# Output projection and second feed-forward product with tokens stationary and 512 weight columns moving

## The chip, the cores and the metric

The kernel runs on one core of one Trainium2 chip. The metric is device time in microseconds (us), the median of a few runs; 2190.91 us for the kernel before, over 3 runs from 2189.48 to 2193.85 us.

## What is computed

Two encoder layers over 256 tokens of 2048 numbers. Each layer runs an input projection, three mixers, an output projection and a feed-forward pair. The two products that the change touches are the one with `w_out` and the one with `w_ff2`:

```python
x = x + jnp.einsum('bse,ed->bsd', y, w_out)      # y: the mixers' outputs, 2048 wide
h = rms_norm(x, norm_ff)
u = jax.nn.relu(jnp.einsum('bsd,df->bsf', h, w_ff1))   # 8192 wide
return x + jnp.einsum('bsf,fd->bsd', u * u, w_ff2)
```

All of it is float32. The kernel keeps that precision on TensorE by cutting every operand in two parts, hi and lo, whose sum is the number, and by adding three products: hi by hi, hi by lo, lo by hi.

## The kernel before, in words

**Weights.** `Weights` (line 212) walks a fixed list of tiles of 128 partitions by 1024 numbers (512 KB). SyncE loads each into `wst` (3 buffers), ScalarE casts it into `whi`, VectorE subtracts to get `wlo` (4 buffers each). `next()` starts the cutting of a tile two tiles ahead of its use.

**Two forms of a large product.** `in_group` (line 362), the input projection, keeps tokens on the PSUM partitions: for each of 16 tiles of the inner dimension (kt) and each of the 2 token tiles (tt), a 128x128 block of the activations is stationary and 512 columns of the weights move, three matmuls of 512 columns. `w_half` (line 386), used for `w_out`, `w_ff1` and `w_ff2`, keeps the output columns on the PSUM partitions: for each kt and each block of 128 output columns, a block of `whi` is stationary while the activations' hi and lo halves (2 x 256 columns side by side) move, and then a block of `wlo` is stationary while the hi half alone moves: one matmul of 512 columns and one of 256.

```python
            mm(c, ps, wh, acts[k0 + k], first and k == 0, end)
            mm(c, ps[:, :S], wl, acts[k0 + k][:, :S], False, False)
```

Below, a *unit* is one kt, 128 tokens and 512 output columns. In the first form it is three matmuls of 512 columns. In the second form a pair (512 and 256 columns) serves 128 output columns of all 256 tokens, half as many outputs as a unit, so a unit is two pairs: four matmuls. Either way 1536 columns move.

**Residual and norms.** `c.x` holds the residual transposed, as 16 tiles of 128 columns by 256 tokens. `out_end` (1005) adds a product's block to it; `ff2_end` (1084) multiplies by the tokens' factor `r2` first. `new_xg` (339) makes from such a tile the next product's operand `xg` (hi on ScalarE, lo on VectorE) and sums squares on GpSimd into `acc`; `square_factor` and `token_factor` sum `acc` over partitions with a small matmul (`ff_r`, `stat`).

**Stages of a layer.** Nine groups of the input projection with the mixers' steps between them; `out_proj` (1015): the first four blocks of columns over the first half of `y`, then over the second, and then the other twelve; four chunks of the feed-forward pair (`ffn`, 1048): 16 blocks of `w_ff1` give 16 tiles `u`, then 16 blocks of `w_ff2` add into x.

**What sets the order.** Each engine runs its instructions in the order in which the Python code issues them. `Stream` (113) keeps a model clock; the mixers' and the ends' steps are generators that `pump()` resumes between two matmuls, when the model says that their operands are there. PSUM has 4 banks for the large products (`g`) and 4 for the rest (`m`). A transpose is a matmul against the identity (line 196).

Of the kernel before, what the change touches and what calls it, by code (L numbers as in the profile page):

```python
# [45 lines left out]
# columns of a layer's vectors  # L46
# [17 lines left out]
# where the MLA heads start: group and weight tile of the input projection  # L64
# [4 lines left out]
class Engine:  # L69
    """An engine's instructions, with an estimate of the time (us) that each one takes."""  # L70
# [141 lines left out]
class Weights:  # L212
    """Weight tiles in the order of their use: loaded and split ahead of it."""
# [13 lines left out]
    def split(self):  # L227
        """hi + lo = w exactly, both in float32r."""
# [27 lines left out]
def weight_order(c, depth):  # L256
    srcs = []
    for l in range(depth):
# [7 lines left out]
        for half in range(2):  # L266
            for i in range(4):
                srcs.append((c.w_out[l, i, half], 1024))
        for i in range(4, KT):
            for half in range(2):  # L270
                srcs.append((c.w_out[l, i, half], 1024))
        for ch in range(NCHUNK):
            for w in (c.w_ff1[l, ch * KT:(ch + 1) * KT], c.w_ff2[l, ch]):
                for i in range(KT):
                    for half in range(2):
                        srcs.append((w[i, half], 1024))
# [11 lines left out]
def rsqrt(c, v, n):  # L288
    """1/sqrt of v [128, n] (n small): exp(-ln(v)/2) and a Newton step."""
# [38 lines left out]
def mm3(c, out, l, r, start, stop):  # L328
    """(l hi + l lo)^T (r hi + r lo) without lo * lo."""
# [9 lines left out]
def new_xg(c, xg, kt, gain):  # L339
    """The next product's operand from x tile kt, and its squares' sum."""  # L340
    nc = c.nc
    hl = tile_xg(c)
    nc.scalar.activation(hl[:, :S], c.x[kt], AF.Copy, scale=gain)
    if kt == 0:
        c.acc = c.small.tile([P, S], F32, tag="acc", name="acc", bufs=1)
        nc.gpsimd.tensor_tensor(out=c.acc, in0=c.x[kt], in1=c.x[kt], op=ALU.mult)
    else:
        sq = c.tmp.tile([P, S], F32, tag="sq", name="sq", bufs=1)
        nc.gpsimd.tensor_tensor(out=sq, in0=c.x[kt], in1=c.x[kt], op=ALU.mult)
# [3 lines left out]
    nc.vector.scalar_tensor_tensor(out=hl[:, S:], in0=c.x[kt], scalar=gain, in1=hl[:, :S].bitcast(F32),  # L353
                                   op0=ALU.mult, op1=ALU.subtract)
    xg[kt] = hl

# [5 lines left out]
def in_group(c, w, hooks=None, prepare=None):  # L362
    """x @ w_in columns: tokens on partitions, [128, w] for each token tile."""
    ps = [c.gps.tile([P, 512], F32, tag="g", name="g") for _ in range(NT)]
    for kp in range(KT // 2):
# [3 lines left out]
        for j in range(2):  # L369
            kt = 2 * kp + j  # L370
            c.s.until(lambda: c.xg[kt])
            wh, wl = hi[:, j * w:(j + 1) * w], lo[:, j * w:(j + 1) * w]
            for tt in range(NT):
                xh = c.xg[kt][:, tt * P:(tt + 1) * P]
                xl = c.xg[kt][:, S + tt * P:S + (tt + 1) * P]
# [25 lines left out]
def token_factor(c, rt):  # L401
    """rsqrt(mean(x^2) + eps) and its negative for each token: [128, 2 * NT]."""
    nc = c.nc
    ps = yield from bank(c, "stat")
    for tt in range(NT):
        mm(c, ps[:, 2 * tt:2 * tt + 2], c.acc[:, tt * P:(tt + 1) * P], c.mean[:, :2], True, True)
    v = c.small.tile([P, 2], F32, tag="tf_v", name="tf_v")
    yield
    nc.vector.tensor_scalar(out=v, in0=ps[:, 0:4:2], scalar1=EPS, scalar2=None, op0=ALU.add)
    c.s.give(m=1)  # L410
# [16 lines left out]
def layer_tables(c):  # L427
    """Rope tables with the layer's gains in them."""
# [18 lines left out]
def latents(c, ps, rt, tf):  # L447
    """Normalised query and key/value latents, transposed and split."""
# [38 lines left out]
def apply_rope(c, out, x, cos, sin, n, rot):  # L487
    """out = x*cos + swap(x)*sin; x, out [128, n, rot] views, tables [128, n, rot]."""
# [11 lines left out]
def k_rope(c, z1):  # L500
# [17 lines left out]
    # hi twice, for a query's hi and lo one above the other, and lo  # L518
# [10 lines left out]
def softmax(c, sc, scale, bias):  # L529
    """softmax(scale * (sc + bias)), keys on partitions, split; sc [128, NT, S] in PSUM."""  # L530
# [50 lines left out]
def mla_head(c, h):  # L581
# [22 lines left out]
    # per token: q nope, k nope, q rope  # L604
# [57 lines left out]
def dil_prep(c, ps, rt, pair):  # L662
    """Two dilated heads, normalised and rotated: columns q0 q1 k0 k1."""
# [62 lines left out]
def ml_gates(c, z1):  # L726
    """Decay sums F, inputs i - F and their running maxima for both directions."""
# [8 lines left out]
    # log_sigmoid(f) = min(f, 0) - log1p(exp(-|f|)); log1p(e) = 2 atanh(e / (2 + e)), a series in (1/3)^2  # L736
# [49 lines left out]
    # rows of hi and lo parts, which the selector adds exactly  # L786
# [19 lines left out]
def ml_qk(c, ps, rt):  # L806
# [7 lines left out]
    for pr in range(2):  # L814
# [6 lines left out]
        # per head: k's hi and lo one above the other, q's hi twice, and q's lo  # L821
# [28 lines left out]
def ml_o(c, ps, rt):  # L850
    """sigmoid(o) times the output norm's gain."""
# [19 lines left out]
def ml_head(c, h):  # L871
# [86 lines left out]
def mixers(c, prepare):  # L958
# [21 lines left out]
    s.spawn(ml_gates(c, z1))  # L980

# [23 lines left out]
def out_end(c, ps, mb, nxt):  # L1005
    nc = c.nc
    yield
    t = c.tmp.tile([P, S], F32, tag="ev1", name="ev1", bufs=3)
    nc.vector.tensor_tensor(out=t, in0=ps[:, S:], in1=c.x[mb], op=ALU.add)
    nc.vector.tensor_tensor(out=c.x[mb], in0=ps[:, :S], in1=t, op=ALU.add)  # L1010
    yield
    yield from new_xg(c, nxt, mb, c.vec[:, V_GF + mb:V_GF + mb + 1])


def out_proj(c):
    nxt = [None] * KT
    G = 4
    ps = [c.gps.tile([P, 512], F32, tag="g", name="g") for _ in range(G)]
    for h in range(2):
        for i in range(G):  # L1020
            w_half(c, c.y, 8 * h, ps[i], h == 0, h == 1)
            if h == 1:
                c.s.spawn(out_end(c, ps[i], i, nxt))
    for mb in range(G, KT):
        p = c.gps.tile([P, 512], F32, tag="g", name="g")
        for h in range(2):
            w_half(c, c.y, 8 * h, p, h == 0, h == 1)
        c.s.spawn(out_end(c, p, mb, nxt))
# [3 lines left out]
def square_factor(c, begin):
    """r^2 = 1 / (mean(x^2) + eps), the same on all partitions."""
    nc = c.nc
    c.r2 = c.small.tile([P, S], F32, tag="r2", name="r2", bufs=1)
    while c.s.clk < begin:
        yield
    ps = yield from bank(c, "ff_r")
    mm(c, ps[:, :S], c.mean, c.acc, True, True)
    yield  # L1040
    nc.vector.tensor_scalar(out=c.r2, in0=ps[:, :S], scalar1=EPS, scalar2=None, op0=ALU.add)
    c.s.give(m=1)
    for h in range(2):
        yield
        nc.vector.reciprocal(c.r2[:, h * P:(h + 1) * P], c.r2[:, h * P:(h + 1) * P])


def ffn(c, l, last_layer):
    """relu(r z)^2 = r^2 relu(z)^2: the tokens' factor r^2 comes after the second product."""
    nc = c.nc  # L1050
    nxt = [None] * KT
    c.s.spawn(square_factor(c, c.s.clk + 12.0))
    for ch in range(NCHUNK):
# [30 lines left out]
def ff2_end(c, ps, db, l, ch, last_layer, nxt):  # L1084
    nc = c.nc
    yield
    t = c.tmp.tile([P, S], F32, tag="ev1", name="ev1", bufs=3)
    nc.scalar.copy(t, ps[:, S:])
    yield
# [12 lines left out]
    yield from new_xg(c, nxt, db, c.vec[:, V_GM + db:V_GM + db + 1])  # L1102
# [190 lines left out]
```

## Time and profile before

| | |
|---|---|
| median of 3 runs | 2190.91 us (2189.48 to 2193.85) |
| span of the profiled execution | 2186.4 us |
| outside the span, against that median | 4.5 us |
| TensorE busy | 99% of the span |
| VectorE, ScalarE, GpSimd busy | 68%, 50%, 10% |
| HBM traffic | 177 GB/s over the span |

The page of the profiled execution gives its span, from the first instruction to the last, and no time of its own beside it; the 4.5 us is the difference to the runs' median. A matmul's recorded duration runs to its modelled end and overlaps the next one's, so what a matmul costs in a stream is the distance from its start to the next start, or a stretch divided by the count of matmuls in it.

### The profile page before, as it was taken

The numbers are of one execution on the slowest core, as the hardware profiler recorded it, in microseconds if no ns is written. First come the engines' busy times: TensorE is split into PE (matmuls) and PEld (weight loads), VectorE is DVE, ScalarE is ACT, GpSimd is POOL, SyncE is SP. The second block draws the span as 40 slices with busy tenths as digits, with TensorE's granted clock in tenths as the row PEclk, the third lists the DMA queues.
The fourth block names the chain that finished last, engine by engine and source line by source line (L and its number), as shares of the span: only waits on it lengthen the run. The fifth ranks groups of instructions, "written<-read, shape, count | busy, mean of one in ns | idle before, by whom it ended". The sixth has DMA issues, their size and how long they took to land.

```text
span 2186.4 us, 31853 instructions
## 1 busy us (share of the span) xinstructions
PE 2156.9 (99%) x12040; PEld 1861.3 (85%) x12040; DVE 1489.3 (68%) x2330; ACT 1100.4 (50%) x1953; POOL 218.5 (10%) x235
## 2 busy tenths in 40 slices
PE   8999999999999999999999999999999999999999
PEld 6788888888888888888887888888888888888887
DVE  7767777666666666667866687776666666666665
ACT  5666654544444444454556666444444444444443
POOL 6112123000000000002411121330000000000000
PEclk9999999999999999999999999999999999999999
DMA  6443445555555555555554334555555555555554
GB/s 229 151 141 119 157 168 185 192 191 184 187 188 186 189 184 191 185 184 199 185 165 158 122 116 164 174 192 192 184 184 192 184 187 188 188 188 185 191 190 157
DMA packets 109882, 387.98 MB, mean 177 GB/s; under 512 B 12448, under 2 KB 14624, under 8 KB 109728
## 3 DMA queue, kind: packets, MB, share of 16 engines
q1 hardware_dynamic: 106848, 382.88, 51.4%
q10 hardware_dynamic: 2880, 3.07, 0.4%
q8 instruction: 94, 1.54, 0.3%
q14 instruction: 60, 0.49, 0.1%
HBM read 383.80 MB, written 2.10 MB: 177 GB/s over the span
## 4 chain that ended last, share of the span: by engine, by line
PE 92%; ACT 3%; POOL 2%; DVE 2%; issue 1%; DMA 0%; POOLq 0%; ACTq 0%
PE g L190 86%; PE mla_z L190 1%; PE mla_s L190 1%; ACT junk L94 1%; POOL acc L94 1%; ACT whi L94 1%; PE oT L190 1%; POOL sq L94 1%; PE ml_h L190 1%; DVE wlo L94 0%; PE ml_st L190 0%; PE pT L196 0%; PE dil_s L190 0%; POOL rp L94 0%; PE dqkT L196 0%
## 5 line engine op out<-in xcount | busy, mean ns | idle before, releaser
L94 DVE TENSOR_TENSOR wlo<-wst,whi 128x1024 fp32r<-128x1024 f32 (+2 forms) x732 | 910.8, 1248 | 255.4 <-ACT whi L94 246.6
L94 ACT CAST whi<-wst 128x1024 fp32r<-128x1024 f32 (+2 forms) x732 | 758.6, 1041 | 371.3 <-PE g L190 292.6
L190 PE MATMUL g<-xg,whi 128*128 128x512 f32 x2048 | 714.5, 398 | 0.0
L190 PE MATMUL g<-u,whi 128*128 128x512 f32 x2048 | 711.0, 394 | 0.0
L190 PE MATMUL g<-u,wlo 128*128 128x256 f32 x2048 | 557.2, 282 | 0.0
L190 PE MATMUL g<-xg,wlo 128*128 128x256 f32 x2048 | 554.2, 281 | 0.0
L190 PEld LDWEIGHTS g<-xg,whi 128*128 128x128 f32 x2048 | 376.7, 188 | 82.5
L190 PEld LDWEIGHTS g<-u,whi 128*128 128x128 f32 x2048 | 376.5, 188 | 77.7
L190 PEld LDWEIGHTS g<-xg,wlo 128*128 128x128 f32 x2048 | 386.6, 189 | 12.6
L190 PEld LDWEIGHTS g<-u,wlo 128*128 128x128 f32 x2048 | 384.9, 188 | 12.4
L190 PE MATMUL g<-whi,xg 128*128 128x512 f32 (+1 forms) x1152 | 373.2, 391 | 6.5 <-ACT whi L94 6.5
L94 ACT COPY ev<-g 128x256 f32<-128x256 f32 x256 | 95.3, 372 | 474.7 <-PE g L190 474.7
L94 DVE TENSOR_TENSOR ev<-g,ev 128x256 f32<-128x256 f32 x256 | 108.6, 424 | 245.9 <-ACT ev L94 245.8
L190 PEld LDWEIGHTS g<-whi,xg 128*128 128x128 f32 x1152 | 215.6, 189 | 45.9 <-ACT whi L94 6.5
L190 PE MATMUL g<-wlo,xg 128*128 128x512 f32 (+1 forms) x576 | 221.9, 385 | 3.5 <-DVE wlo L94 3.3
L190 PE MATMUL g<-y,whi 128*128 128x512 f32 x512 | 178.4, 395 | 0.0
L190 PE MATMUL g<-y,wlo 128*128 128x256 f32 x512 | 139.3, 282 | 0.0
L190 PEld LDWEIGHTS g<-wlo,xg 128*128 128x128 f32 x576 | 109.1, 189 | 23.4 <-DVE wlo L94 6.9
L190 PEld LDWEIGHTS g<-y,whi 128*128 128x128 f32 x512 | 94.1, 188 | 19.3
L190 PEld LDWEIGHTS g<-y,wlo 128*128 128x128 f32 x512 | 96.3, 188 | 3.0
L94 POOL TENSOR_TENSOR sq<-x 128x256 f32<-128x256 f32 x60 | 78.2, 1303 | 126.4 <-DVE x L94 125.2
L94 ACT ACTIVATE xg<-x,vec 128x256 fp32r<-128x256 f32 x64 | 31.6, 508 | 86.8 <-DVE x L94 84.5
(199 smaller groups left out, 1353.2 us busy)
## 6 DMA issues: line engine op xcount, KB each, us to landing
wst<-w_ff SPq DMA_DIRECT2D x512, 512.0 KB, 3.2
wst<-w_in SPq DMA_DIRECT2D x128, 512.0 KB, 3.5
wst<-w_out SPq DMA_DIRECT2D x64, 512.0 KB, 3.2
wst<-w_in SPq DMA_DIRECT2D x16, 336.0 KB, 2.8
wst<-w_mla SPq DMA_DIRECT2D x12, 416.0 KB, 3.3
x<-xT SPq DMA_DIRECT2D x8, 256.0 KB, 5.3
out<-x ACTq DMA_DIRECT2D x16, 128.0 KB, 3.1
vec<-vecs ACTq DMA_DIRECT2D x2, 468.0 KB, 4.5
```

The lines of the kernel that those rows point to most:

```text
L94: return fn(*args, **kw)
L190: c.nc.tensor.matmul(out, lhsT, rhs, start=start, stop=stop)
```

## The change

`w_out` and `w_ff2` go over to the token-stationary form (`token_group`, made out of `in_group`); `w_ff1` stays in `w_half`. The residual is kept as 2 tiles of 128 tokens by 2048 columns. A group is now 512 columns of both token tiles in two PSUM banks, accumulated over all kt (the output projection's first two groups take the first half of `y` first). The end of a group is one VectorE operation for each token tile; in `ff2_end` the tokens' factor is a scalar per partition. `next_xg` takes the place of `new_xg`: ScalarE squares with a running sum, TensorE transposes each 128x128 block through a PSUM bank, and ScalarE and VectorE cut the result in hi and lo with the gain. The first norm still reads `xT`, now through borrowed buffers; the token-major copy of x (2 loads of 1 MB) is read behind the second group of the input projection. The output leaves in token order.

```diff
-def new_xg(c, xg, kt, gain):
+def next_xg(c, xg, g, ss, col):
+    nc = c.nc
+    for tt in range(NT):
+        j = c.tmp.tile([P, 512], F32, tag="junk5", name="junk5", bufs=1)
+        nc.scalar.activation(j, c.x[tt][:, g * 512:(g + 1) * 512], AF.Square, accum_out=ss[:, tt, g:g + 1])
+    for half in range(2):
+        kt = 4 * g + 2 * half
+        tp = yield from bank(c, "xT")
+        for i in range(2):
+            for tt in range(NT):
+                transpose(c, tp[:, i * S + tt * P:i * S + (tt + 1) * P], c.x[tt][:, (kt + i) * P:(kt + i + 1) * P])
+        yield
+        hls = [tile_xg(c) for i in range(2)]
+        split_gains(c, hls, tp, col + kt)
+        c.s.give(m=1)
+        xg[kt:kt + 2] = hls
+        yield
...
+def token_group(c, acts, ps, w, kps=range(KT // 2), hooks=None, prepare=None):
+    for kp in kps:
...
         hi, lo = c.w.next()
         for j in range(2):
             kt = 2 * kp + j
...
             for tt in range(NT):
...
                 mm(c, ps[tt][:, :w], xh, wh, kt == 0, False)
                 mm(c, ps[tt][:, :w], xh, wl, False, False)
                 mm(c, ps[tt][:, :w], xl, wh, False, kt == KT - 1)
...
 def mixers(c, prepare, after):
...
     s.spawn(ml_gates(c, z1))
+    if after:
+        after()
...
-def out_end(c, ps, mb, nxt):
+def out_end(c, ps, g, ss, nxt):
     nc = c.nc
+    cols = slice(g * 512, (g + 1) * 512)
     yield
-    t = c.tmp.tile([P, S], F32, tag="ev1", name="ev1", bufs=3)
-    nc.vector.tensor_tensor(out=t, in0=ps[:, S:], in1=c.x[mb], op=ALU.add)
-    nc.vector.tensor_tensor(out=c.x[mb], in0=ps[:, :S], in1=t, op=ALU.add)
+    for tt in range(NT):
+        nc.vector.tensor_tensor(out=c.x[tt][:, cols], in0=ps[tt], in1=c.x[tt][:, cols], op=ALU.add)
     yield
-    yield from new_xg(c, nxt, mb, c.vec[:, V_GF + mb:V_GF + mb + 1])
+    yield from next_xg(c, nxt, g, ss, V_GF)
...
-        for db in range(KT):
-            ps = c.gps.tile([P, 512], F32, tag="g", name="g")
-            for half in range(2):
-                w_half(c, us, 8 * half, ps, half == 0, half == 1)
-            c.s.spawn(ff2_end(c, ps, db, l, ch, last_layer, nxt))
+        for g in range(NX):
+            ps = two_banks(c)
+            token_group(c, us, ps, 512)
+            c.s.spawn(ff2_end(c, ps, g, l, ch, last_layer, nxt))
...
-    nc.scalar.copy(t, ps[:, S:])
-    yield
-    nc.vector.tensor_tensor(out=t, in0=ps[:, :S], in1=t, op=ALU.add)
-    nc.vector.tensor_tensor(out=t, in0=t, in1=c.r2, op=ALU.mult)
-    nc.vector.tensor_tensor(out=c.x[db], in0=c.x[db], in1=t, op=ALU.add)
+    for tt in range(NT):
+        nc.vector.scalar_tensor_tensor(out=c.x[tt][:, cols], in0=ps[tt], scalar=c.r2[:, tt:tt + 1],
+                                       in1=c.x[tt][:, cols], op0=ALU.mult, op1=ALU.add)
...
+    def load_tokens():
+        for tt in range(NT):
+            nc.sync.dma_start(c.x[tt], x[tt])
```

**How the order moves, first place.** TensorE at the start of the first chunk's second product, before the change (`g` is the PSUM bank, `u` the activations, `whi` and `wlo` the weights' parts; the operands are written in the program's order and not by which is stationary):

```order
L190 MATMUL g_4884<-u_4139,whi_4833 128x512
L190 MATMUL g_4884<-u_4139,wlo_4834 128x256
L190 MATMUL g_4884<-u_4192,whi_4833 128x512
L190 MATMUL g_4884<-u_4192,wlo_4834 128x256
L190 MATMUL g_4884<-u_4253,whi_4833 128x512
L190 MATMUL g_4884<-u_4253,wlo_4834 128x256
```

The same place with the change:

```order
L193 MATMUL g_4728<-whi_4677,u_3988 128x512
L193 MATMUL g_4728<-wlo_4678,u_3988 128x512
L193 MATMUL g_4728<-whi_4677,u_3988 128x512
L193 MATMUL g_4729<-whi_4677,u_3988 128x512
L193 MATMUL g_4729<-wlo_4678,u_3988 128x512
L193 MATMUL g_4729<-whi_4677,u_3988 128x512
L193 MATMUL g_4728<-whi_4677,u_4040 128x512
```

One `u` tile took a pair in each of sixteen blocks; it now takes six matmuls of 512 columns in each of four groups, three in either bank. Nothing stands between them.

**Second place.** TensorE with the change in the first product of the feed-forward pair, right behind the output projection of layer 0 (`xg_3917`, `xg_3918`, `xg_3935`, `xg_3936` are the operand's tiles kt 12 to 15, `xT` the bank of the transposes, `x_90` and `x_91` the residual):

```order
L193 MATMUL g_3871<-xg_3917,whi_3852 128x512
L193 MATMUL g_3871<-xg_3917,wlo_3853 128x256
L193 MATMUL g_3871<-xg_3918,whi_3852 128x512
L193 MATMUL g_3871<-xg_3918,wlo_3853 128x256
L199 MATMUL xT_3930<-const_92,x_90 128x128
L199 MATMUL xT_3930<-const_92,x_91 128x128
L199 MATMUL xT_3930<-const_92,x_90 128x128
L199 MATMUL xT_3930<-const_92,x_91 128x128
L193 MATMUL g_3871<-xg_3935,whi_3852 128x512
L193 MATMUL g_3871<-xg_3935,wlo_3853 128x256
L193 MATMUL g_3871<-xg_3936,wlo_3853 128x256
L193 MATMUL g_3871<-xg_3936,whi_3852 128x512
```

ScalarE at that place, from the last group's end on:

```order
L97 ACTIVATE junk5_3895,xss_3135<-x_90 128x512
L97 ACTIVATE junk5_3897,xss_3135<-x_91 128x512
L97 CAST whi_3906<-wst_3837 128x1024
L97 ACTIVATE xg_3917<-xT_3899,vec_88 128x256
L97 ACTIVATE xg_3918<-xT_3899,vec_88 128x256
L97 ACTIVATE xg_3935<-xT_3930,vec_88 128x256
L97 ACTIVATE xg_3936<-xT_3930,vec_88 128x256
```

Before the change these sixteen products stood in a row with no transposes among them. Now the last four transposes stand directly ahead of the matmuls that need their result; the four ahead of those (`xT_3899`) stand behind the first matmuls of kt 6.

**Third place.** SyncE with the change, at the third group of the input projection of layer 0:

```order
L227 DMA wst_522<-w_in 128x1024
L227 DMA wst_539<-w_in 128x1024
L227 DMA wst_569<-w_mla 128x832
L1208 DMA x_90<-x 128x2048
L1208 DMA x_91<-x 128x2048
L227 DMA wst_593<-w_in 128x1024
L227 DMA wst_644<-w_in 128x1024
```

The two loads of the residual stand between the first weights of an attention head and the fifth tile of that group.

## Rows read from the trace of the kernel before

**Rows 1.** The page: span, busy time by engine, granted clock in 40 slices.
```profile
span 2186.4 us, 31853 instructions
...
PE 2156.9 (99%) x12040; PEld 1861.3 (85%) x12040; DVE 1489.3 (68%) x2330; ACT 1100.4 (50%) x1953; POOL 218.5 (10%) x235
...
PEclk9999999999999999999999999999999999999999
```

**Rows 2.** The page, chain that ended last: share of the span by line.
```profile
PE g L190 86%; PE mla_z L190 1%; PE mla_s L190 1%; ACT junk L94 1%; POOL acc L94 1%; ACT whi L94 1%; PE oT L190 1%; POOL sq L94 1%; PE ml_h L190 1%; DVE wlo L94 0%; PE ml_st L190 0%; PE pT L196 0%; PE dil_s L190 0%; POOL rp L94 0%; PE dqkT L196 0%
```

**Rows 3.** TensorE's waits in the whole span: total us, times, longest us.
```profile
PE g L190 <- DVE wlo L94: 3.3, 6, 0.8
```

**Rows 4.** Chain, three stretches (w_ff2, w_out, input projection): start, us, what, instructions.
```profile
477.94 82.10 PE g L190 x467
...
299.78 80.35 PE g L190 x457
...
1098.82 20.19 PE g L190 x89
```

**Rows 5.** Timeline of TensorE in the w_ff2 product: start us, us, instruction.
```profile
530.12 0.39 PE L190 MATMUL g<-u,whi 128*128 128x512 f32 x1
530.35 0.28 PE L190 MATMUL g<-u,wlo 128*128 128x256 f32 x1
530.47 0.39 PE L190 MATMUL g<-u,whi 128*128 128x512 f32 x1
```

**Rows 6.** Timeline of TensorE, four transposes between matmuls of the input projection.
```profile
83.16 0.40 PE L190 MATMUL g<-whi,xg 128*128 128x512 f32 x1
83.40 0.60 PE L196 MATMUL nkT<-const,nk 128*128 128x128 f32 x4
...
84.07 0.39 PE L190 MATMUL g<-wlo,xg 128*128 128x512 f32 x1
```

**Rows 7.** Timeline of TensorE around the small matmul of square_factor.
```profile
389.48 0.28 PE L190 MATMUL g<-xg,wlo 128*128 128x256 f32 x1
...
390.25 0.28 PE L190 MATMUL g<-xg,wlo 128*128 128x256 f32 x1
```

**Rows 8.** Groups by form, whole span: count, busy us, mean ns, idle before.
```profile
L94 DVE TENSOR_TENSOR wlo<-wst,whi 128x1024 fp32r<-128x1024 f32 x704 | 884.5, 1259 | 243.8 <-ACT whi L94 235.2
L94 ACT CAST whi<-wst 128x1024 fp32r<-128x1024 f32 x704 | 736.0, 1050 | 349.3 <-PE g L190 279.4 <-DMA wst<-w_in 26.4 <-DVE x L94 26.1
...
L94 DVE TENSOR_TENSOR p_lo<-pT,p_hi 128x512 fp32r<-128x512 f32 x24 | 16.2, 681 | 18.4 <-ACT p_hi L94 18.4
...
L94 ACT ACTIVATE dil_z<-g,rt 128x512 f32<-128x512 f32 x12 | 7.7, 699 | 0.0
...
L196 PE MATMUL nkT<-const,nk 128*128 128x128 f32 x48 | 7.2, 272 | 0.0
...
L94 DVE SCALAR_TENSOR_TENSOR mla_k<-nkT,vec,mla_k 128x256 fp32r<-128x256 f32 x12 | 5.7, 475 | 0.0
L94 ACT ACTIVATE mla_k<-nkT,vec 128x256 fp32r<-128x256 f32 x12 | 5.7, 474 | 0.0
```

**Rows 9.** DMA at its fullest; then SyncE's and ScalarE's timelines near 60 us.
```profile
22.00:26.00 4.00, 3.58 (x16) 2.28 (x14) 4.00 (x5) 1.05 (x1) 3.77 (x4) 1.00 0.97 388
...
53.58 0.33 SPq L224 DMA_DIRECT2D wst<-w_mla  x1
57.46 0.33 SPq L224 DMA_DIRECT2D wst<-w_in  x1
...
60.93 1.05 ACT L94 CAST whi<-wst 128x1024 fp32r<-128x1024 f32 x1 [1.74 <-DMA wst<-w_in]
```

**Rows 10.** The last pieces of the chain, then the page's weight loads.
```profile
2181.90 0.38 ACT ev L94
...
2183.22 0.43 DVE x L94
...
wst<-w_ff SPq DMA_DIRECT2D x512, 512.0 KB, 3.2
```

More of the change, by code (lines that the diff above doesn't have):

```diff
@@ L34 @@
 NG = 8
+NX = D // 512
+OUT_ORDER = [(g, range(4 * h, 4 * h + 4)) for h in range(2) for g in range(2)] + [(g, range(8)) for g in (2, 3)]
 C_ID, C_MEAN, C_ONE, C_TRIU, C_TRIL = (i * P for i in range(5))
@@ L265, in weight_order @@
                 srcs += [(c.w_mla[l, h], 832) for h, at in enumerate(MLA_AT) if at == (g, kp)]
-        for half in range(2):
[L267 to L271, printed above, removed]
+        srcs += [(c.w_out[l, g, kp], 1024) for g, kps in OUT_ORDER for kp in kps]
         for ch in range(NCHUNK):
[L273 to L276, printed above, removed]
+            srcs += [(c.w_ff1[l, ch * KT + i, half], 1024) for i in range(KT) for half in range(2)]
+            srcs += [(c.w_ff2[l, ch, g, kp], 1024) for g in range(NX) for kp in range(KT // 2)]
     return srcs
@@ L352, in new_xg, with two_banks @@
     yield
-    nc.vector.scalar_tensor_tensor(out=hl[:, S:], in0=c.x[kt], scalar=gain, in1=hl[:, :S].bitcast(F32),
+    nc.vector.scalar_tensor_tensor(out=hl[:, S:], in0=src, scalar=gain, in1=hl[:, :S].bitcast(F32),
                                    op0=ALU.mult, op1=ALU.subtract)
     xg[kt] = hl
+def next_xg(c, xg, g, ss, col):
[15 more added lines that the diff above has]
+        yield
 def tile_xg(c):
     return c.xp.tile([P, 2 * S], F32R, tag="xg", name="xg", bufs=KT)
-def in_group(c, w, hooks=None, prepare=None):
-    ps = [c.gps.tile([P, 512], F32, tag="g", name="g") for _ in range(NT)]
-    for kp in range(KT // 2):
+def two_banks(c):
+    return [c.gps.tile([P, 512], F32, tag="g", name="g") for _ in range(NT)]
+def token_group(c, acts, ps, w, kps=range(KT // 2), hooks=None, prepare=None):
+    for kp in kps:
         if prepare:
@@ L403, in token_factor @@
     nc = c.nc
-    ps = yield from bank(c, "stat")
-    for tt in range(NT):
-        mm(c, ps[:, 2 * tt:2 * tt + 2], c.acc[:, tt * P:(tt + 1) * P], c.mean[:, :2], True, True)
     v = c.small.tile([P, 2], F32, tag="tf_v", name="tf_v")
-    yield
-    nc.vector.tensor_scalar(out=v, in0=ps[:, 0:4:2], scalar1=EPS, scalar2=None, op0=ALU.add)
-    c.s.give(m=1)
+    if c.xss is None:
+        ps = yield from bank(c, "stat")
+        for tt in range(NT):
+            mm(c, ps[:, 2 * tt:2 * tt + 2], c.acc[:, tt * P:(tt + 1) * P], c.mean[:, :2], True, True)
+        yield
+        nc.vector.tensor_scalar(out=v, in0=ps[:, 0:4:2], scalar1=EPS, scalar2=None, op0=ALU.add)
+        c.s.give(m=1)
+    else:
+        yield
+        mean_square(c, v, c.xss)
     y = yield from rsqrt(c, v, 2)
@@ L1002, in mixers, with new_ss, square_factor @@
     s.spawn(dil_v(c, ps, rt, slice(256, 768)))
-def out_end(c, ps, mb, nxt):
+def new_ss(c):
+    return c.small.tile([P, NT, NX], F32, tag="xss", name="xss")
+def out_end(c, ps, g, ss, nxt):
     nc = c.nc
+    cols = slice(g * 512, (g + 1) * 512)
     yield
-    t = c.tmp.tile([P, S], F32, tag="ev1", name="ev1", bufs=3)
-    nc.vector.tensor_tensor(out=t, in0=ps[:, S:], in1=c.x[mb], op=ALU.add)
-    nc.vector.tensor_tensor(out=c.x[mb], in0=ps[:, :S], in1=t, op=ALU.add)
+    for tt in range(NT):
+        nc.vector.tensor_tensor(out=c.x[tt][:, cols], in0=ps[tt], in1=c.x[tt][:, cols], op=ALU.add)
     yield
-    yield from new_xg(c, nxt, mb, c.vec[:, V_GF + mb:V_GF + mb + 1])
+    yield from next_xg(c, nxt, g, ss, V_GF)
 def out_proj(c):
     nxt = [None] * KT
[L1017 to L1028, printed above, removed]
+    ss = new_ss(c)
+    ps, ends = {}, []
+    for g, kps in OUT_ORDER:
+        if g not in ps:
+            ps[g] = two_banks(c)
+        token_group(c, c.y, ps[g], 512, kps)
+        if kps[-1] == KT // 2 - 1:
+            ends.append(c.s.spawn(out_end(c, ps[g], g, ss, nxt)))
     c.xg = nxt
[L1032 to L1036, printed above, removed]
+    c.s.spawn(square_factor(c, ss, ends))
+def square_factor(c, ss, ends):
+    c.r2 = c.small.tile([P, NT], F32, tag="r2", name="r2")
+    while not all(t.over for t in ends):
         yield
-    ps = yield from bank(c, "ff_r")
-    mm(c, ps[:, :S], c.mean, c.acc, True, True)
     yield
[L1041 to L1045, printed above, removed]
+    mean_square(c, c.r2, ss)
+    c.nc.vector.reciprocal(c.r2, c.r2)
 def ffn(c, l, last_layer):
@@ L1101, in ff2_end, with encoder @@
     yield
-    yield from new_xg(c, nxt, db, c.vec[:, V_GM + db:V_GM + db + 1])
+    yield from next_xg(c, nxt, g, c.xss, V_GM)
 @with_exitstack
-def encoder(ctx, tc, xT, const, vecs, w_in, w_in1, w_mla, w_out, w_ff1, w_ff2, out):
+def encoder(ctx, tc, xT, x, const, vecs, w_in, w_in1, w_mla, w_out, w_ff1, w_ff2, out):
     nc = tc.nc
@@ L1132, in encoder @@
     rest = load_vectors(c, 0)
-    xall = c.xp.tile([P, KT, S], F32, tag="x", name="x")
-    c.x = [xall[:, i] for i in range(KT)]
+    c.x = [c.xp.tile([P, D], F32, tag="x", name="x", bufs=NT) for _ in range(NT)]
+    c.xss = None
+    xts = []
     c.const = c.cp.tile([P, C_ALL], F32, tag="const", name="const")
@@ L1178, in encoder @@
     c.identr, c.masks, c.sel = cr[:, 0:P], cr[:, P:3 * P], cr[:, 3 * P:3 * P + 64]
+    def load_tokens():
+        for tt in range(NT):
+            nc.sync.dma_start(c.x[tt], x[tt])
     for l in range(depth):
-        mixers(c, prepare if l == 0 else None)
+        mixers(c, prepare if l == 0 else None, load_tokens if l == 0 else None)
         out_proj(c)
@@ L1246, in blocks @@
             n, m // P, kk // 1024, P, 1024)
-    put["w_out"] = blocks(a["w_out"])
+    cols512 = lambda t: np.stack([pairs(t[:, :, g * 512:(g + 1) * 512]) for g in range(NX)], 1)
+    put["w_out"] = cols512(a["w_out"])
     put["w_ff1"] = blocks(a["w_ff1"])
-    put["w_ff2"] = blocks(a["w_ff2"]).reshape(depth, KT, NCHUNK, 2, P, 1024).transpose(0, 2, 1, 3, 4, 5)
+    put["w_ff2"] = np.stack([cols512(a["w_ff2"][:, i * D:(i + 1) * D]) for i in range(NCHUNK)], 1)
     cols = lambda t: t.reshape(depth, -1, P).transpose(0, 2, 1)
```

54 lines of the change are left out of this document (29 added, 25 removed).

## Prediction

> **What bounds the kernel now.** I read the page's busy shares first: TensorE is busy 99% of the span, VectorE 68%, ScalarE 50%, GpSimd 10%, and the granted clock stands in the top tenth (the 2.4 GHz level) in all 40 slices [rows 1]. Busy is no proof, so I read the chain that ended last: 86% of the span is TensorE on the large products (`g`) [rows 2]. Then TensorE's waits: in the whole span the large products wait 3.3 us for `wlo`, in six pieces [rows 3]. So time comes off only if TensorE issues the same work faster, and whatever the change adds to TensorE's queue comes on.
>
> The question is therefore what a matmul costs in a stream. A chain stretch with nothing but large products gives it as its length over its count [rows 4]. In the `w_ff2` product 467 matmuls take 82.10 us, 175.8 ns each, so a pair (512 and 256 columns) costs 351.6 ns. In the output projection 457 take 80.35 us, the same 351.6 ns a pair. In layer 1's first input group, which is already in the form that the change brings, 89 matmuls of 512 columns take 20.19 us: 226.9 ns each. The timeline shows inside a pair that the 512 columns take 530.12 to 530.35, about 230 ns, and the 256 columns 120 ns [rows 5]: the narrow one costs more than half of a wide one.
>
> **The change, part by part.**
>
> *Both products.* A unit (defined ahead) costs 2 x 351.6 = 703.2 ns now and 3 x 226.9 = 680.7 ns in the new form, 22.5 ns less. `w_ff2` has 2 layers x 4 chunks x 16 kt x 4 groups x 2 token tiles = 1024 units, `w_out` 2 x 16 x 4 x 2 = 256. 1280 x 0.0225 = **28.8 us less**. The new form's moving operands are the same `whi` and `wlo` tiles as in the row I take the price from; only the stationary block comes from `u` or `y`, not from `xg`. The ends are 226.9 ns and the 236 ns to which single wide matmuls round in a timeline; I take 226.9, since it is the mean of a long unbroken run, which the new product also is.
>
> *Transposes, added to TensorE.* Three norms read the residual through them (both feed-forward norms, and layer 1's first): 3 x 32 = 96, in 24 groups of four. From 83.16 to 84.07 stand two wide matmuls and one such group [rows 6]: 0.91 - 2 x 0.227 = 0.456 us. 24 x 0.456 = **11.0 us more**. Ends: 11 and 12 (0.5 us a group).
>
> *Small matmul of `square_factor`, removed.* From 389.48 to 390.25 a wide and a narrow matmul and this one take 0.77 us [rows 7], 0.42 over a pair. Twice: **0.8 us less**. The `stat` matmuls of layer 1 go too; with well under 1 us they are left at nothing.
>
> *Squares, evictions.* GpSimd's squares go; ScalarE gets 24 squares of 128x512. A group's end falls from ScalarE and VectorE steps on each of 16 blocks to two VectorE operations in each of four groups. None of these engines bounds the stage: a weight tile costs VectorE 1.26 us and ScalarE 1.05 us [rows 8], and it will be used up in 12 x 0.227 = 2.72 us, now 8 x 0.352 = 2.81 us. Cost nothing, covered by TensorE's stream; without that cover each chunk would show its own waits on `wlo`.
>
> *Weight supply.* A load lands in 3.2 us [rows 10]; with cast and subtraction a `wst` buffer turns round in some 5.5 us, and there are three, so a tile could come every 1.85 us. The stretch of rows 4 at 226.9 ns a matmul ran on this supply. Nothing.
>
> *Hand-over from the output projection to the feed-forward pair, a new wait, twice.* Before, the last block's tile was kt 15 alone, and about 5 us of cover stood ahead of it. Now the last group yields kt 12 to 15 together. Take T as the end of its last matmul. VectorE adds the second token tile by T+0.9 (0.68 us [rows 8]; the first one's bank is done 0.7 us before T). ScalarE's queue then holds two squares (0.70 us for an operation of that shape [rows 8]; 0.9 with the reading of the sum is my estimate; to T+2.0), a weight cast (T+3.05), and two cuts of 0.47 us [rows 8], to T+4.4 with their waits; VectorE's halves follow to T+5.0. TensorE, with one group of transposes in its first seven pairs, wants kt 12 at T+4.7: nearly hidden. But the last four transposes stand behind kt 13, to about T+5.9; ScalarE's cut takes to T+6.5, VectorE's to T+7.1, the next tile's 0.5 more. TensorE stands idle 1.2 and then 0.3 us, 1.5 in all. Behind the waiting matmul stands the rest of its queue, so it is all on the path: **3.0 us more** for two layers. Ends: nothing, if all engines are ahead, and 8 (4 each, if a weight cast and a subtraction get ahead of a cut again).
>
> Layer 1's first norm has no such wait: its input group needs kt 12 only after 12 x 6 x 0.227 = 16 us.
>
> *The token-major copy of x.* Two loads of 1 MB stand on SyncE's queue ahead of the tile whose load was issued at 57.46; ScalarE already waited 1.74 us for that tile's landing [rows 9]. At the fullest rate seen, 388 GB/s [rows 9], 2.1 MB take 5.4 us. They can start when SyncE has issued the head's weights, at 53.58 and some tenths, so 3.5 of the 5.4 us are over when the tile's load is issued and 2 lie ahead of it. I take **1.5 us more**, a little under that, since a split tile is needed only some time after its cast; ends 0 and 5.4.
>
> *End.* The last block's end now runs through ScalarE and three VectorE operations, 2181.90 to 2183.65 [rows 10]; one VectorE operation of about 0.7 us takes its place, and the last store is twice as large. **0.7 us less**; ends 0 and 1.0.
>
> **Sum.** -28.8 + 11.0 - 0.8 + 3.0 + 1.5 - 0.7 = -14.8 us. The page gives the profiled execution's span alone, 2186.4 us, 4.5 below the median of the runs; the sum is a difference and is taken off the median: 2190.9 - 14.8 = **2176 us**. All gains with the low costs: -28.8 + 11.0 - 0.8 - 1.0 = -19.6, 2171. The high costs: -28.8 + 12 - 0.8 + 8 + 5.4 = -4.2, 2187.
>
> **Rivals.**
>
> *A matmul's price is its columns (slower).* Both forms move 1536 columns. At a pair's price per column, 351.6/768 = 0.458 ns, a unit stays at 703 ns, the gain is nothing, and the other terms (+14.0) decide: 2205 us. For it: the counts are equal. Against it: the 89 wide matmuls at 226.9 ns are 0.443 ns a column [rows 4]. By the Trainium skill, "TensorE: Matmul & The Clock Gate", section "Wait — 56ns, not 53.3ns?", a warm matmul starts N/2.4 + about 2.5 ns after the last; the one matmul saved would then give 2.5 ns a unit, 3.2 us in all, and the time would be an estimated 2202 us. The trace disagrees: 226.9 ns where that gives 215.8, and 351.6 ns for a pair where it gives 325. Chance 4%.
>
> *The wide stream in the new place is no faster than wide matmuls now (slower).* If each of them took 240 ns behind `u` or `y`, a unit would cost 720 ns, 16.8 more: +21.5 + 14.0, 2226 us. The point at which it decides is 230.9 ns: there a unit saves 10.9 ns, just what the other terms cost. For it: wide matmuls in pairs are spaced 230 to 240. Against it: those stand behind a narrow one, and the row of 89 has none. Chance 5%.
>
> *A transpose costs its whole record (no change).* Its mean record is 272 ns [rows 8]. 96 x 0.272 = 26.1 in place of 11.0: 2191 us. The Trainium skill, same page, section "Part 4: PE-mode transpose", has ~275 ns in one kernel's context. The record agrees, but four of them fit in 0.60 us [rows 6], so they overlap. Chance 3%.
>
> *The new waits come at their upper ends.* Hand-over 8 and x 5.4: 2186 to 2187 us. For it: the four cuts stand on engines that also feed the weights. Against it: at both places I let no other work run ahead of the waiting step. Chance 10%.
>
> *The change doesn't do what it says*: TensorE's listing shows three wide matmuls a unit and 24 groups of transposes, so I give this nothing of its own.
>
> **Chances.** The forecast has 78%. Within 0.2% (4.4 us, about what a measurement of this kernel can tell from no change) lies 2186.5 to 2195.3: the transposes' rival and nearly half of the upper ends, 7%. Slower: both column rivals, 8% with rounding. Faster: 85%. The range takes the bounds of the costs, 2170 to 2187; it leaves out the slower rivals and the no-change one.
>
> **What would show it.** In the profile after: `g<-whi,u` and `g<-wlo,u` in long chain stretches at 226 to 228 ns a matmul; 96 `xT` matmuls, about 0.46 us a group; two waits of 1 to 2 us of `g` on VectorE's `xg` at the start of each feed-forward stage; one cast near 60 us that waits some 2 us longer for its load; no waits on `wlo` in the chunks. I am wrong if the wide stream is above 230 ns, if `wlo` waits appear in each group, or if TensorE idles over 4 us at a hand-over.

## Result and profile after

The changed kernel takes **2201.78 us** (median of 4 runs, 2200.01 to 2203.68) beside 2190.19 us for the kernel before on the same chip (4 runs): ratio 1.0052, 95% interval 1.0037 to 1.0066. It is slower by half a per cent; the forecast was 2176. The span of the profiled execution grew from 2186.4 to 2197.9 us, by 11.5. Every run on record lies some 2 us above its own span, not 4.5, and the spans of the kernel before go from 2186.0 to 2191.8 us, so that a difference of a few us between two single spans says little by itself.

The page of the kernel after: its span and busy times, the chain by line, two groups of matmuls (out<-in, shapes, count | busy us, mean ns | idle before) and the loads of `x` (count, KB each, median us to landing). The first lines answer to [rows 1] and [rows 2]:

```profile
span 2197.9 us, 28890 instructions
...
PE 2164.0 (98%) x10848; PEld 1805.4 (82%) x10848; DVE 1326.9 (60%) x1963; ACT 1077.9 (49%) x1873; POOL 110.9 (5%) x142
...
PE g L193 85%; PE mla_z L193 1%; ACT whi L97 1%; PE mla_s L193 1%; ACT junk L97 1%; POOL acc L97 1%; DMA wst<-w_in 1%; PE oT L193 1%; POOL sq L97 1%; DVE wlo L97 1%; PE ml_h L193 1%; PE xT L199 0%; PE ml_st L193 0%; PE pT L199 0%; PE dil_s L193 0%
...
L193 PE MATMUL g<-whi,u 128*128 128x512 f32 x2048 | 646.0, 395 | 0.0
...
L193 PE MATMUL g<-wlo,u 128*128 128x512 f32 x1024 | 404.5, 395 | 0.0
...
x<-x SPq DMA_DIRECT2D x2, 1024.0 KB, 7.9
```

TensorE issues 1192 matmuls fewer and is busy 7 us longer. VectorE fell from 68% to 60% and GpSimd from 10% to 5%; neither bounds anything. The idle time ahead of the matmuls on `u` is 0.0, so the new stream never waits. It is slow while it runs, which the chain shows in two stretches of the kernel after (start us, us, what, instructions), first `w_ff2`, then `w_out` with the first transposes; they answer to [rows 4]:

```profile
479.79 75.37 PE g L193 x323
```

```profile
297.02 29.98 PE g L193 x129
327.00 0.44 PE xT L199 x4
327.44 4.89 PE g L193 x21
332.33 0.44 PE xT L199 x4
```

75.37 us over 323 is **233.3 ns a wide matmul on `u`**, and 29.98 over 129 is 232.4 on `y`, where the forecast took 226.9. A unit costs 699.9 and 697.2 ns against 703.2 before: 1024 x 3.3 + 256 x 6.0 = 4.9 us saved, not 28.8. A group of four transposes takes 0.44 us. TensorE's waits in the whole span (us in all, times, longest), for [rows 3] and the hand-over:

```profile
PE g L193 <- ACT whi L97: 6.7, 1, 6.7
PE dqkT L199 <- POOL dil_z L97: 4.4, 4, 1.2
PE g L193 <- DVE wlo L97: 3.8, 7, 1.2
PE g L193 <- DVE xg L97: 2.9, 2, 1.4
```

The first two stood in the kernel before as well, at 6.5 and 4.4 us; the last is new.

Where the time went by stage, in us, from the first to the last large matmul of each stage in the traces (e1 and e11 are experiments below):

| stage | before | after | e1 | e11 |
|---|---|---|---|---|
| end of layer 0's input projection | 283.1 | 286.3 | 284.7 | 283.0 |
| `w_out`, layer 0 | 93.8 | 95.9 | 93.9 | 95.2 |
| `w_ff1`, chunk 0, layer 0 | 90.8 | 93.1 | 93.1 | 92.7 |
| `w_ff1`, chunk 1, layer 0 | 90.5 | 90.5 | 90.6 | 90.0 |
| `w_ff2`, chunk 0, layer 0 | 90.1 | 89.7 | 87.2 | 87.2 |
| `w_ff2`, chunk 3, layer 0 (six groups of transposes) | 90.1 | 92.3 | 90.1 | 90.2 |
| layer 1's input projection | 268.8 | 269.3 | 269.3 | 268.2 |

In e11 the input projection ends 1.7 us earlier than in e1 and `w_out` takes 1.3 us longer: some of the mixers' last steps run inside `w_out` there.

Each chunk of `w_ff2` should have become 128 x 22.5 ns = 2.9 us shorter, and became 0.4 shorter.

### The profile page after: what moved, and what is told of

Its sections match the earlier page's. It is cut to its first block, busy times and chain, and to the rows that moved or that the text cites. A ratio compares the mean times of both kernels' runs of the same rounds, so it can differ in the third digit from the quotient of the medians.

```text
span 2197.9 us, 28890 instructions
## 1 busy us (share of the span) xinstructions
PE 2164.0 (98%) x10848; PEld 1805.4 (82%) x10848; DVE 1326.9 (60%) x1963; ACT 1077.9 (49%) x1873; POOL 110.9 (5%) x142
## 4 chain that ended last, share of the span: by engine, by line
PE 91%; ACT 3%; DVE 2%; POOL 2%; issue 1%; DMA 1%; POOLq 0%; ACTq 0%; SPq 0%; DVEq 0%
PE g L193 85%; PE mla_z L193 1%; ACT whi L97 1%; PE mla_s L193 1%; ACT junk L97 1%; POOL acc L97 1%; DMA wst<-w_in 1%; PE oT L193 1%; POOL sq L97 1%; DVE wlo L97 1%; PE ml_h L193 1%; PE xT L199 0%; PE ml_st L193 0%; PE pT L199 0%; PE dil_s L193 0%
## 5 line engine op out<-in xcount | busy, mean ns | idle before, releaser
L193 PE MATMUL g<-whi,u 128*128 128x512 f32 x2048 | 646.0, 395 | 0.0
L193 PEld LDWEIGHTS g<-whi,u 128*128 128x128 f32 x2048 | 384.5, 188 | 92.7
L193 PE MATMUL g<-wlo,u 128*128 128x512 f32 x1024 | 404.5, 395 | 0.0
L193 PEld LDWEIGHTS g<-wlo,u 128*128 128x128 f32 x1024 | 192.3, 188 | 46.2
L193 PE MATMUL g<-whi,y 128*128 128x512 f32 x512 | 165.2, 397 | 0.0
L97 DVE TENSOR_TENSOR ev<-g,ev 128x256 f32<-128x256 f32 x128 | 54.3, 424 | 132.3 <-ACT ev L97 132.3
L193 PEld LDWEIGHTS g<-whi,y 128*128 128x128 f32 x512 | 96.5, 188 | 21.8
L193 PE MATMUL g<-wlo,y 128*128 128x512 f32 x256 | 101.0, 395 | 0.0
L97 DVE SCALAR_TENSOR_TENSOR ev<-ev 128x256 f32<-128x256 f32 x128 | 54.5, 426 | 4.4
L193 PEld LDWEIGHTS g<-wlo,y 128*128 128x128 f32 x256 | 48.3, 189 | 10.4
```

The costliest lines, as they stand in the source:

```text
L97: return fn(*args, **kw)
L193: c.nc.tensor.matmul(out, lhsT, rhs, start=start, stop=stop)
```

## Experiments

The three products whose matmuls are now wide in the same way differ in one thing that the code shows: where in SBUF the stationary tile lies against the weight tile that streams. The pools are laid out in the order in which `encoder` opens them: `xp` (49152 bytes a partition), `wp` (45056), `big` (16512), `half` (9216), then `t2` with `u` and `y`. A tile of `xg`, `u` or `y` is 2048 bytes, a weight tile 4096, so all of `xg` and of the weights lie 0 apart modulo 2048. Between `wp` and `t2` stand 16512 + 9216 = 25728 bytes, 1152 modulo 2048 and 128 modulo 256. So in the input projection the two operands are 0 apart, and in the changed products 128 apart modulo 256. The kernel before has the same distances. **Theory A**: this distance sets the price. **Theory B**: it isn't addresses; the price comes with the way the stream starts or with its stage (what other engines and DMA do there). **Theory C**: tiles that don't begin on 128 bytes (all begin at 96 modulo 128) cost it.

**e1_same_residue**: only the order of the pools.

```diff
+    c.big = pool("big", 4)
+    c.half = pool("half", HALF)
     c.xp = pool("xp", 1)
     c.wp = pool("wp", 1)
-    c.big = pool("big", 4)
-    c.half = pool("half", HALF)
     c.t2 = pool("t2", T2)
```

> The changed kernel with the SBUF pools in another order (the mixers' pools ahead of the operand and weight pools): the operand tiles xg, the weight tiles whi and wlo and the tiles u and y now all start at the same address modulo 2048 bytes (1888); in the changed kernel xg and the weights start at 736 and u and y at 1888. Nothing else moves. Theory A (what counts is how the stationary tile's address lies to the moving one's): the second product's wide matmuls fall from 233.4 ns to the 226.7 ns of the input group, 1280 units x 3 x 6 ns = 23 to 26 us off the time, near 2177 us. Theory B (the stream falls into one of several rhythms by the way it starts, whatever the addresses): 233 ns stay, 2202 us. Theory C (each tile begins 96 bytes behind a multiple of 128 and costs a 128-byte piece more): no change, 2202 us.

Measured: 2175.71 us (2174.78 to 2177.64), ratio 0.9933 (0.9916 to 0.9949). The stretch of `w_ff2` over the same 75 us, in e1, and then in e7, whose distance is 64:

```profile
479.88 75.25 PE g L193 x332
```

```profile
479.82 75.37 PE g L193 x323
```

The first is 226.7 ns a matmul, the price that the forecast took, the second 233.3. With that price comes the forecast's time: 2190.9 - 14.8 = 2176.1 had been worked out, 2175.7 came. The program has the same 28890 instructions as the kernel after.

**e2_cross_residue**: the order `xp, big, half, wp, t2`, which leaves `u` and `y` 0 from the weights and puts `xg` 128 from them modulo 256.

> The changed kernel with the mixers' pools between the operand pool and the weight pool: weights, u and y start at 1888 modulo 2048 and xg alone at 736. Theory A: the second product and the output projection fall to 226.7 ns a wide matmul, and the input groups rise from 226.7 to some 233 ns: 1280 x 3 x 6.5 ns = 25 us less against 1728 x 6.5 ns = 11 us more, near 2188 us. Theory B: both stay, 2202 us. Theory C: no change.

Measured: 2177.63 us (2174.69 to 2179.28), ratio 0.9939 (0.9924 to 0.9954), 10 us below the 2188 of theory A. The last pieces of the chain in e2 from 1096 to 1116, layer 1's first input group; the same group's piece in e1; and the `w_ff1` stretch of e2 from 570 to 645:

```profile
1097.09 4.89 PE g L193 x21
1101.99 0.44 PE xT L199 x4
1102.42 13.71 PE g L193 x59
```

```profile
1103.01 13.18 PE g L193 x58
```

```profile
569.80 75.31 PE g L193 x429
```

The input group has risen from 227.2 ns in e1 to 13.71/59 = 232.4, while `w_ff2` stays at e1's 75.25 us for 332, 226.7 ns: the price has moved with the distance and not with the stage, so B falls. Two things were not foreseen. The two input projections became only 1.5 and 2.0 us longer than in e1, 3.5 instead of 11; why so little of the price reaches their length isn't shown. And the pairs of the first FFN product, where `xg` is the operand that streams, fell to 2 x 75.31/429 = 351.1 ns; over the same 75 us e1 has 426 matmuls, 353.3 a pair, and over 2048 pairs that is 4.5 us. Together, 7.5 and 4.5 us, they cover the 10. **Of the two distances tried with pairs, they want the one that wide streams don't.** Before the change, `w_ff2` ran as pairs at 128 modulo 256 and cost 351.6 [rows 4]. So the change took the product from the distance that suits pairs and left it at the one that doesn't suit wide matmuls.

**e3_after_128** and **e4_before_128**: 32 unused bytes ahead of everything in the kernel after and in the kernel before, so that all tiles begin on 128 bytes and no distance changes.

```diff
+    c.cp.tile([P, 8], F32, tag="pad", name="pad", bufs=1)
```

> The changed kernel with one unused tile of 32 bytes per partition ahead of the large tiles, so that xg, wst, whi, wlo, u and y start at a multiple of 128 bytes, where all of them started 96 bytes behind one; the distances among them stay as they were. Theory C: 226.7 ns is 17 x 13.33 ns, and 512 float32 numbers are 16 pieces of 128 bytes that touch 17 when they start inside one; aligned, a wide matmul falls to about 213 to 216 ns and a narrow one from 120 to about 107 ns. Then the units cost some 645 ns in both products, and the pairs of the first feed-forward product 325 instead of 353 ns: in all about 5000 wide matmuls less 12 to 18 ns and 2048 pairs less 28 ns, over 120 us, near 2070 us. Theory A and B: no change, 2202 us.

> The kernel before with the same 32 unused bytes per partition. Theory C: its pairs fall from 351.6 to about 325 ns, 4608 pairs x 26 ns = 120 us, and its input groups' 1536 wide matmuls by 12 ns, 18 us: near 2050 to 2060 us; and since a unit then costs 650 ns as pairs and 647 ns as wide matmuls, the changed form gains nothing and pays for its transposes, so that this kernel beats the aligned changed one by about 10 us. Theories A and B: no change, 2190 us.

Measured: 2200.56 us, ratio 1.0045 (1.003 to 1.006), with 75.13 us for 322 matmuls, 233.3 ns; and 2191.27 us, ratio 1.0002 (0.9993 to 1.0011), with 75.28 us for 428 matmuls of `w_ff2`, 351.8 ns a pair. C falls.

**e5_apart_1280, e6_apart_128, e7_apart_64**: which distances serve. e5 puts 128 unused bytes between `wp` and `big` (1280 apart, a multiple of 256 and not of 2048), e6 opens `half` ahead of `xp` (128 apart), e7 is e1 with 64 unused bytes ahead of `t2`.

> The changed kernel with 128 unused bytes between the weights' pool and the mixers' pools: u and y now start 1280 bytes behind the weights modulo 2048, instead of 1152; xg and weights stay 0 apart. A stationary block is 512 bytes of a row, taken at 0, 512, 1024 or 1536 in its tile, so only the distance modulo 512 can count: 128 in the changed kernel, 256 here. If any multiple of 256 is as good as 0, the second product falls to 226.8 ns a wide matmul and the time to about 2176 us; if the distance has to be 0 modulo 512, wide matmuls stay above 230 ns and the time near 2202 us. By theory B (rhythm by the start alone) no change, 2202 us.

> The first experiment's kernel with another order of the same pools, so that u and y start 128 bytes behind the weights modulo 2048 (128 modulo 512, as in the changed kernel, at another distance in SBUF), xg and weights 0 apart. If the distance modulo 512 (or 256) sets the price: 232 to 234 ns a wide matmul in both moved products, near 2200 us, as in the changed kernel. If what the first experiment mended was something else in the pools' order, 227 ns and 2176 us.

> The first experiment's kernel with 64 unused bytes ahead of the pool of u and y: 64 bytes behind the weights, xg and weights 0 apart. If a coarse step such as 128 or 256 bytes counts, the price rises above 230 ns and the time to 2195 or 2200 us; if any multiple of 64 serves, 227 ns and 2176 us stay.

Measured, with the wide matmul in the stretch from 480 to 555:

| | apart, modulo 256 | us | ratio | wide matmul on `u` |
|---|---|---|---|---|
| after | 128 (1152) | 2201.78 | 1.0052 | 75.37/323 = 233.3 ns |
| e6 | 128 | 2200.11 | 1.0044 (1.0028 to 1.006) | 75.13/322 = 233.3 |
| e7 | 64 | 2202.82 | 1.0049 (1.0033 to 1.0065) | 75.37/323 = 233.3 |
| e5 | 0 (1280) | 2178.59 | 0.994 (0.9923 to 0.9958) | 75.25/332 = 226.7 |
| e1 | 0 | 2175.71 | 0.9933 (0.9916 to 0.9949) | 75.25/332 = 226.7 |

A multiple of 256 bytes serves, 64 and 128 beyond one don't.

**e8_repaired**: e1, the first two blocks of `w_ff1` by halves in each chunk (so that kt 12 to 15 are wanted later), and the load of `x` two input groups later.

```diff
+FF1_ORDER = [(i, h) for h in range(2) for i in range(2)] + [(i, h) for i in range(2, KT) for h in range(2)]
```

> The first experiment's kernel (addresses equal modulo 2048) with two more edits: the first two blocks of w_ff1 in each chunk run over the first half of the operand, then both over the second (as the output projection's first groups do), which gives the hand-over 2.8 us more cover; and the token-major copy of x is loaded two groups later. Two waits of about 1.5 us at the hand-overs and the wait of 1.6 us near 65 us go: 2175.7 - 4.5 = about 2171 us. If the hand-over waits only move to the second block, 2174 us.

Measured: 2180.48 us (2179.21 to 2181.44), ratio 0.995 (0.9932 to 0.9968): 4.8 us above e1. Both waits went as meant: the hand-over's fell from 2.9 to 1.5 us for the two layers, and the one near 65 us is gone. But at its new place the load did more harm: between 136 and 146 us TensorE falls another 5.4 us behind the kernel before, with a wait of 2.5 us (`pT` for `sm_e`) and granted clocks of 0.80 and 0.50 in the slices of 4 us from 140 to 148. Near 104 us it lost 3.0 us more to a lower clock, see the last section.

**e9_more_transposes**: e1 with each transpose issued twice, so that the 96 added ones are priced by themselves.

```diff
-        for i in range(2):
+        for i in (0, 1, 0, 1):
```

> Base: the version with xg, weights and u, y all at one residue (e1_same_residue, 2175.7 us). Every one of the 96 transposes is issued twice into the same bank (192 in all), nothing else changes, so the run prices the transposes by themselves. Forecast's term (a group of four costs TensorE 0.456 us, starts 109 ns apart): 24 x 4 x 0.109 = +10.5 us, 2186. Rival, each costs its whole record of 272 ns: 96 x 0.272 = +26, 2202. Rival, they fit into idle time of TensorE: 0, 2176. At the two hand-overs the second four may add up to 0.5 us of wait each.

Measured: 2188.13 us (11 runs), ratio 0.9992 (0.9983 to 1.0001), beside 0.9933 for e1: 0.0059, or 12.9 us; by the spans, 2183.8 - 2173.5 = 10.3 us. Its group of transposes (count | busy, mean ns), then one group of now eight in the chain (start us, us):

```profile
L199 PE MATMUL xT<-const,x 128*128 128x128 f32 x192 | 24.9, 272 | 0.0
```

```profile
324.55 0.87 PE xT L199 x8
```

Records of 272 ns as in [rows 8], but eight take 0.87 us where four took 0.44, 109 ns each on the path; 10.3 us for 96 is 107 ns, and 12.9 us would be 134. The rivals of the whole record (+26) and of no cost are out.

**e10_ff1_order**: e8's first edit alone, on e1.

> Base e1_same_residue (2175.7 us) with one of e8's two edits alone: in each chunk the first two blocks of w_ff1 go by halves, so that kt 12 to 15 are wanted some 2.8 us later; the load of x stays where the change put it. If the hand-over's wait is what this hides: 0.8 to 2 us less per layer, 2172 to 2174. If the order of the first two blocks costs something elsewhere, or the wait only moves behind other work: 2175 to 2177. A stretch of half clock near 104 us (seen in some kernels and not in others) would put 1.7 us on either.

Measured: 2176.72 us (2174.59 to 2180.18), ratio 0.9938 (0.9926 to 0.9951): no difference from e1 that can be told. In its waits the hand-over has halved, as meant:

```profile
PE g L194 <- DVE xg L98: 1.5, 2, 0.8
```

That is 1.4 us for the two layers, below what the runs can tell.

**e11_ff1_pairs_apart**: e1 with the feed-forward `xg` alone 128 bytes further into a longer slot, which gives the first FFN product's pairs the distance that they want.

```diff
-T2, HALF = 22, 7
+T2, HALF = 20, 7
-        hls = [tile_xg(c) for i in range(2)]
+        hls = [tile_xg(c, 32 if col == V_GF else 0) for i in range(2)]
-def tile_xg(c):
-    return c.xp.tile([P, 2 * S], F32R, tag="xg", name="xg", bufs=KT)
+def tile_xg(c, at=0):
+    return c.xp.tile([P, 2 * S + 64], F32R, tag="xg", name="xg", bufs=KT)[:, at:at + 2 * S]
```

> Base e1_same_residue. The normed tiles of the feed-forward stage, and they alone, are put 128 bytes further into a longer slot (2304 bytes; two fewer slots in the pool of u and y pay for it), so in the first FFN product the moving xg stands 128 modulo 256 from its stationary weights, while the input groups and both changed products keep 0. In e2_cross_residue that distance went with pairs of 350.6 ns in place of 353.0. If the distance is the cause there as well: 2048 pairs x 2.4 ns = 4.9 us less, 2171, with pairs near 350.6 and input groups still at 227. If the pairs in e2 were cheaper for another reason: 353 and 2176. If the two slots are missed: waits of g on u, over 2176.

**e12_both**: e10 and e11 together.

> e10_ff1_order and e11_ff1_pairs_apart together. If both edits hold and don't touch each other: 2171 less 0 to 3 us, 2168 to 2171, over 1% under the kernel before. If only the distance holds: as e11. If neither: 2176.

Measured: e11 2172.14 us (2170.24 to 2176.17), ratio 0.9919 (0.9906 to 0.9931); e12 2172.2 us (2169.79 to 2178.29), ratio 0.9917 (0.9903 to 0.9932). The stretch of `w_ff1` from 570 to 645 in e11, then in e1:

```profile
569.87 75.31 PE g L193 x429
```

```profile
569.84 75.25 PE g L193 x426
```

351.1 ns a pair against 353.3, and the span is 5.2 us under e1's, where 4.9 were expected (the medians give 3.6). By the stages, 0.4 us in the first chunk of each layer and 0.6 in each of the other six make 4.4. Its input groups stay at the low price (1100.16 to 1116: 15.94 us for 75 large products, some of them of the next, narrower group). e11 and e12 are the fastest versions found, 18 us (0.8%) under the kernel before; that e12 gains over e11 isn't shown.

## Why the prediction was wrong

**The failed step is the price of the wide matmul in the new place.** The text took 226.9 ns, on the ground that "only the stationary block comes from `u` or `y`, not from `xg`". That was the difference that decided: `u` and `y` lie 128 bytes off modulo 256 from the weights, and at that distance the trace has 233.3 and 232.4 ns. The second rival (the wide stream in the new place no faster) had a break-even that held, 230.9 ns (its own terms give 230.8), but was given 5%, because its only evidence was taken to be the matmuls' spacing inside pairs. The row that could have warned is in [rows 4]: it is from one pair of tiles alone, the input group's, and no row before has `u` or `y` as the stationary operand. The text named 236 ns as the other end and then left it out of the range; 9.1 ns x 3 x 1280 would have been 35 us.

That the first rival's time came nearly true is chance. It gave 2205 us, or 2202 by the estimate beside it, since the same columns were to cost the same; 2201.78 was measured. The unit came to 699.9 ns, near the 703.2 of pairs, because of where its blocks lie: in e1 the same columns cost 680.1 ns, so columns alone don't set the price. Two small slips in the text's sums change nothing: 24 x 0.456 is 10.9, and the two new waits at their upper ends come to 2185 us and not 2186 to 2187.

The Trainium skill, "TensorE: Matmul & The Clock Gate", Part 2, section "Step-by-step: what each phase is for", has the stationary operand and the stream on two independent read ports, so that loading the next block takes nothing from the running matmul. Here the loads run beside the matmuls (busy 82% and 98% of the span), but the matmuls' price is not independent of where the blocks lie: 226.7 or 233.3 ns for the same instructions in e1 and after. Where the Trainium skill and this measurement differ, the measurement decides.

The other terms, each against its measure:

- Both products: -28.8 forecast; -4.9 measured. In e1, with the price as forecast, 1280 units x (3 x 226.7 - 703.2 ns) = -29.6.
- Transposes: +11.0; +10.3 by e9's span, and 24 x 0.44 = 10.6 from the chain. Right.
- Hand-over: +3.0, in each layer a wait of 1.2 and one of 0.3; 2.9, one wait of some 1.4 in each layer. Right in its sum.
- Small matmul: -0.8, not isolated. In chunk 0 of `w_ff1` the stage grew by 2.3, where a wait of 1.4 and two groups of transposes (0.9) alone give 2.3, so nothing of it shows.
- The load of `x`: +1.5; 1.6 in the kernel after. Counted by the large matmuls of layer 0's input projection, TensorE is 0.2 us ahead of the kernel before at the 231st (near 62 us) and 1.6 behind at the 241st (near 70), and the 1.6 stay to the projection's end, where another 1.6 of half clock have joined them (below). The sign that was named is there: the cast that started at 60.93 after a wait of 1.74 [rows 9] starts at 63.94 after one of 5.20. From the waits of the kernel after between 50 and 75 us:

```profile
ACT whi L97 <- PE ml_F L193: 5.2, 1, 5.2
DVE wlo L97 <- ACT whi L97: 2.1, 1, 2.1
PE ml_aT L199 <- DVE ml_na L97: 1.6, 1, 1.6
```

  The first is put down to TensorE, but in e1 the same cast's 5.19 us are put down to its load, and in e8, which loads `x` later, it starts at 60.71 after 1.78. VectorE waits for the cast and does the step `ml_na` behind it, and TensorE waits for that; the kernel before has no such wait. In e10, e11 and e12 TensorE is 0.9 to 1.1 us behind at the same place. Right, and by the way that the text gave, though the cast waits 3.5 us longer and not 2.
- End: -0.7; the last large matmul ends 4.5 us ahead of the end before and 4.0 after, so -0.5 (the chain's last piece after is `DVE x` for 1.45 us).
- Weight supply, squares, evictions: nothing forecast. `g` waits 3.8 us for `wlo` instead of 3.3 [rows 3], and none of it in the wide stretches. Right.

Sum as measured, with the 1.6 of half clock that no term has: -4.9 + 10.6 + 2.9 + 1.6 - 0.5 + 1.6 = +11.3, of the 11.5 by which the span grew. The change's costs came as forecast, but for the small matmul; its gain was there to be had, and five sixths of it was lost to 128 bytes.

## What to carry to other kernels

A matmul's price read from one stream holds for another only if its operands lie alike: before moving a product onto other tiles, work out from the pools how far the stationary tile is from the streaming one, and treat a distance that no row shows as an unknown price. Here wide matmuls were faster at a multiple of 256 bytes (2.9%) and pairs of 512 and 256 columns at 128 beyond one (0.6%), and either cost only the order of pools or a little padding. When a new stream never waits and yet is slow, vary addresses as well.

## What the runs showed of the hardware

The distance effect is the surprise: 226.7 against 233.3 ns (2.9%) for wide matmuls with a new stationary block each, 353.3 against 351.1 (0.6%) the other way for pairs. That it is the distance and not the place is shown by e1, e2, e5, e6 and e7; why a distance costs (what collides) isn't shown by any run. Only 0, 64 and 128 modulo 256 were tried, and with pairs only 0 and 128.

A smaller one: the kernel after loses some 1.6 us near 104 us without a wait. Busy time by engine in two slices (window, us, PE, PEld, DVE, ACT, POOL, then granted clock, DMA share, GB/s), kernel after, then e1:

```profile
100.00:104.00 4.00, 2.12 (x13) 1.29 (x12) 3.50 (x9) 1.68 (x4) 0.00 (x0) 1.00 0.39 131
104.00:108.00 4.00, 4.00 (x23) 4.00 (x22) 1.74 (x3) 3.00 (x7) 0.00 (x0) 0.57 0.02 6
```

```profile
100.00:104.00 4.00, 2.13 (x13) 1.31 (x12) 3.51 (x9) 1.69 (x4) 0.00 (x0) 1.00 0.35 131
104.00:108.00 4.00, 4.00 (x34) 3.87 (x34) 1.84 (x4) 3.29 (x10) 0.00 (x0) 1.00 0.03 6
```

After a slice in which TensorE was busy 2.12 of 4 us, the granted clock was 0.57 of full speed in the next, so most of that slice ran at the lower of the two levels (1.2 of 2.4 GHz); 4 x 0.43 is 1.7 us. In e1 the slice ahead is alike and the clock stayed at 1.00 there, as it did before and in e2, e9, e10, e11 and e12; e5 and e6 show 0.57 too, e3, e4 and e7 fall as well, and e8 shows 0.68 and 0.50 from 100 to 108. Such a stretch stands elsewhere in some traces: e1 has 0.59 from 64 to 68, e10 0.59 from 1180 to 1184. What tips it stays open; the page's row of the clock, in slices of 55 us, shows none of it.

The program doesn't fix it: where the mean granted clock of the kernel before is 1.000 its span is 2186.0 to 2186.5 us, and where it is 0.998, 2189.1 to 2191.8. So differences of two or three us among e1, e2, e5 and e10 are not told apart. The distance effect is not this: e5 and e6 both fall to 0.57 near 104 us, and their spans are 2175.7 and 2198.0 us.
